# A two-layer fp16 kernel on one core: second-product operations on ScalarE in halves of 384 columns, no kept x sums, new orders

## The chip, the core and the metric

The kernel runs on one core of a Trainium2 chip. TensorE (PE) multiplies, VectorE (DVE) and ScalarE (ACT) do element-wise work and move results out of the PSUM banks, GpSimd (POOL) and SyncE (SP) issue most of the DMA transfers, and TensorE's weight loads (PEld) run beside its matmuls. The metric is the device time of one execution in microseconds. Lower is better. The kernel before was timed three times: 878.06, 879.29 and 879.67 us.

## The reference

```python
# x: 16 x 512 x 768, w1: 768 x 3072, b1: 3072, w2: 3072 x 768, all float32
y = np.matmul(x, w1) + b1
y = np.maximum(y, 0)
return np.matmul(y, w2).astype(np.float32)
```

As one matrix, x has 8192 rows. The two products are 8192 x 768 by 768 x 3072 and 8192 x 3072 by 3072 x 768.

## The kernel before

**Tiling.** The work is cut into 16 iterations: two chunks of the hidden dimension (1536 columns of w1, 1536 rows of w2) times eight blocks of 1024 rows of x. Iterations 0 to 7 go through the blocks with the first chunk and write their results to the output, iterations 8 to 15 go through them again with the second chunk and add to it. `SECOND_CHUNK` gives the order of blocks in the second pass.

**Bilinear products.** Both products are done by a scheme like Strassen's. Instead of all block products of the plain scheme, sums and differences of blocks are multiplied, and sums of the results give the output. Products are fp16 with fp32 sums in PSUM. In each iteration the first product (`add_first`, TensorE line L1013) is 40 products of six matmuls of 128x128 by 128x256, the second product (`add_second`, L1142) 26 products of six matmuls of 128x128 by 128x384. Iteration 0 computes its first product plainly (`first_block`, L923). The operands that are sums are made on DVE: sums of x at L768, of w1 at L784, of w2 at L802, of y (the hidden layer) at L986. The tables at the head of the file (`X_SUMS`, `SECOND_OPS`, ...) say which.

**Banks and operations.** A second product fills a pair of PSUM banks, 384 columns in each. Its six matmuls are three steps h for each of two banks j, with j as the inner loop, so that they alternate between the banks. An *operation* then takes the pair on, for one of three ends. A *seed* writes it, with a sign, into another pair of banks, where later products add to it, a *sum* keeps it in SBUF, and an *out* is a finished piece of output. Operations that add a kept sum run on DVE (L1159, and L1056, L1059, L1064 in the first product), those that only copy or negate run on ScalarE (L1153, and L1049, L1053 in the first product), one instruction of 128x768 each in the second product.

**Slots.** Kept sums and outs lie in nine SBUF slots, called s in the profile. The slot of an out becomes free when its store has landed. Stores go out plainly on SyncE (L1189) in the first chunk and accumulating on GpSimd (L1191) in the second. An out that adds a kept sum can be *apart*: the sum is stored by itself (L1194), ScalarE alone copies the product's part, and the store of that part accumulates on GpSimd. `SPLIT` names outs that are apart in every iteration, `APART` iterations in which all are.

**x and the weights.** GpSimd loads x with a cast to fp16 (xn, L648), ScalarE squares it for a check of ranges (L708), SyncE transposes it by DMA (L700, the *turns*, eight for each block), and DVE makes the sums of x. Block 2 is kept (`KEPT`): in iteration 2 its x and sums are also stored to DRAM (xd, SyncE L721, 20 transfers of 192 KB), and in iteration 8 they are loaded from there for iteration 9 (L728), which needs no turns and no sums of x. The second chunk's weights are cast to DRAM by GpSimd in iterations 2 to 6 (w1d L627, w2d L633), 18 transfers, and loaded by SyncE in iteration 7 (L1363, L1403); the sums of w1 and w2 for the second chunk follow.

**What sets the order.** `plan` adds all of this as tasks with an engine, a cost in ns and dependencies. `Graph.run`, a list scheduler, gives each engine its order from these costs, from latencies between engines (`CROSS`) and from due times that TensorE's product order sets (`FIRST_ORDER`, `SWITCH_ORDER` for iterations 7 and 8, `SECOND_ORDER`, `LAST_ORDER`). Each engine then runs its instructions in that order, and waits at each for what it reads and for the place that it writes.

Of the kernel before, what the change touches and what calls it, by code (L numbers as in the profile page):

```python
# [31 lines left out]
X_SUMS = ((15, 2, 1, -1), (21, 7, 1, -1), (16, 1, 0, -1), (9, 6, 5, -1), (20, 7, 5, -1), (12, 2,  # L32
    0, -1), (14, 3, 5, -1), (11, 2, 5, -1), (8, 4, 5, -1), (17, 6, 1, -1), (10, 3, 1, -1), (22, 6,
    7, -1), (23, 4, 6, -1), (13, 0, 6, -1), (18, 3, 2, -1), (19, 4, 2, -1))
FIRST_U = (8, 9, 21, 18, 2, 13, 20, 19, 1, 14, 10, 17, 11, 22, 6, 12, 5, 23, 15, 16)
W1_SUMS = ((7, 0, 1, 1), (6, 2, 5, 1), (9, 6, 3, -1), (12, 9, 0, -1), (14, 7, 9, -1), (11, 5, 4,
    -1), (8, 6, 4, -1), (13, 7, 2, -1), (10, 8, 7, -1), (15, 3, 5, -1), (16, 3, 10, -1), (17, 1,
# [31 lines left out]
FIRST_ORDER = (16, 0, 12, 36, 20, 8, 4, 7, 9, 1, 18, 24, 3, 15, 10, 28, 32, 38, 6, 21, 14, 35, 17,  # L69
    30, 11, 27, 34, 37, 29, 13, 31, 23, 2, 26, 25, 5, 22, 39, 33, 19)  # L70
SWITCH_ORDER = (16, 0, 12, 36, 20, 4, 9, 8, 7, 18, 24, 3, 1, 10, 15, 28, 21, 38, 6, 14, 32, 35,
    17, 11, 30, 27, 34, 5, 13, 29, 26, 31, 37, 2, 23, 25, 22, 39, 19, 33)

Y_SUMS = ((17, 5, 9, 1), (21, 11, 10, 1), (41, 8, 9, 1), (24, 4, 0, 1), (16, 8, 12, 1), (20, 0, 3,
# [4 lines left out]
SECOND_U = (36, 38, 25, 27, 28, 10, 16, 23, 15, 2, 13, 39, 20, 35, 34, 17, 42, 41, 29, 33, 43, 40,  # L79
    18, 22, 32, 31)  # L80
W2_SUMS = ((11, 2, 1, -1), (9, 7, 6, -1), (14, 9, 3, -1), (8, 1, 5, -1), (20, 9, 5, -1), (17, 3,
    11, 1), (10, 4, 7, -1), (24, 11, 10, -1), (18, 7, 3, -1), (12, 1, 0, -1), (15, 8, 2, -1), (16,
    8, 0, -1), (13, 3, 10, 1), (22, 16, 4, -1), (25, 0, 13, 1), (19, 6, 15, -1), (23, 12, 9, -1),
# [41 lines left out]
    5, 24, 20)  # L125
LAST_ORDER = (13, 15, 4, 17, 10, 8, 12, 18, 3, 0, 1, 2, 14, 19, 23, 21, 11, 16, 25, 7, 9, 5, 22,
    6, 24, 20)
LAST_FOLD = (6,)
LAST_DIRECT = (0, 1, 2, 3, 5)
LAST_POOL = ()  # L130

X_FUSE = (0,)
# [387 lines left out]
SPLIT = (6,)  # L520
# [954 lines left out]
```

## Time and profile before

| | us |
|---|---|
| three runs | 878.06, 879.29, 879.67 |
| profiled execution, own time | 878.07 |
| its span | 876.5 |
| PE busy | 850.6 (97%) |
| DVE busy | 744.5 (85%) |
| ACT busy | 557.8 (64%) |
| POOL busy | 154.7 (18%) |
| DMA, mean rate over the span | 164 GB/s |

The profiled execution lies at the quick end of the three runs. "Busy" is time within instructions, and PE's ends are modelled, since matmuls are pipelined. A window row gives, for a stretch of the span, each engine's busy time and instruction count, the granted TensorE clock (1.00 is full) and the share of the 16 DMA engines' time that transfers took, which can exceed 1. In rows of groups, the figures after the bar are the total busy time, the mean ns of one, and the engine's idle time just before them with what ended most of it. In rows of waits they are total us, count and the longest. In rows of the timeline they are start, duration, engine, line and operation, with the idle time before it and what ended that in brackets.

### The profile page before, as it was taken

To read this page: it belongs to the slowest core of one execution; us is meant where nothing else is said; L and a number is where in the kernel's file an instruction comes from. 1 tells how busy PE (TensorE), PEld (TensorE's weight loads), DVE (VectorE), ACT (ScalarE), POOL (GpSimd) and SP (SyncE) were. 2 spreads that over 40 slices of the span, in tenths; PEclk is the share of its full clock that TensorE was granted. 3 is DMA by queue.
4 is the path that set the end of the run, shared out by engine and by line. 5 is a ranking of instruction groups with operands and counts; after the bars stand their busy time and mean duration, and the time that the engine had idled before them with its cause. 6 is when DMAs were issued, how large, how long until landed. Compare 5 with 4: busy or idle time off the path is not lost. (4 is left out here: it accounts for less than half of the span.)

```text
span 876.5 us, 16636 instructions
## 1 busy us (share of the span) xinstructions
PE 850.6 (97%) x6381; PEld 625.0 (71%) x6381; DVE 744.5 (85%) x1206; ACT 557.8 (64%) x1066; POOL 154.7 (18%) x166
## 2 busy tenths in 40 slices
PE   8997998899999999998999999999999999999996
PEld 7556767577685877867677586776858677686873
DVE  5895995888989899897999969899798988989886
ACT  5866775676767676675766348777747667355462
POOL 5212020020200101010030311405032140401301
PEclk9999999999999999999999999999999999999999
DMA  9999679496683959657595564958887895965746
GB/s 212 200 196 204 145 153 270 84 238 106 152 171 72 220 91 195 113 125 218 162 232 166 85 107 72 202 83 146 146 134 124 153 145 98 145 111 64 127 108 146
DMA packets 166550, 129.71 MB, mean 148 GB/s; under 512 B 87852, under 2 KB 164932, under 8 KB 166468
## 3 DMA queue, kind: packets, MB, share of 16 engines
q0 software_dynamic: 53872, 64.89, 46.8%
q1 hardware_dynamic: 112128, 62.74, 28.4%
q8 instruction: 50, 0.82, 0.4%
q10 hardware_dynamic: 468, 1.00, 0.3%
q14 instruction: 32, 0.26, 0.1%
HBM read 73.54 MB, written 69.99 MB: 164 GB/s over the span
## 5 line engine op out<-in xcount | busy, mean ns | idle before, releaser
L1142 PE MATMUL ps<-v,y 128*128 128x384 f16 x2496 | 416.8, 326 | 2.3 <-ACT ps L1153 0.7
L1013 PE MATMUL ps<-x,v 128*128 128x256 f16 x3600 | 398.1, 273 | 14.0 <-ACT ps L1049 4.1
L1013 PEld LDWEIGHTS <-v 128*128 128x128 f16 x3600 | 352.1, 98 | 59.0 <-issue 16.7
L1142 PEld LDWEIGHTS <-y 128*128 128x128 f16 x2496 | 243.7, 98 | 171.4 <-issue 15.0
L986 DVE TENSOR_TENSOR y<-y 128x768 f16<-128x768 f16 (+1 forms) x368 | 222.4, 639 | 6.6 <-DVE y L1056 0.5
L1056 DVE CUSTOM_DVE_ANT_0 y<-ps,s 128x512 f16<-128x512 f32 x240 | 160.1, 687 | 37.0 <-ACT s L1053 15.9
L1153 ACT ACTIVATE s<-ps 128x768 f32<-128x768 f32 x171 | 138.4, 810 | 81.7 <-PE ps L1142 65.3
L1053 ACT ACTIVATE s<-ps,bt 128x256 f32<-128x256 f32 x180 | 74.8, 473 | 81.5 <-PE ps L1013 72.2
L1191 POOL DMA_DIRECT2D out_dram<-s x79 | 95.5, 1419 | 141.6 <-ACT s L1153 62.7
L768 DVE TENSOR_TENSOR x<-x 128x768 f16<-128x768 f16 (+1 forms) x195 | 108.1, 577 | 9.2 <-DMA x<-xn 8.0
L1053 ACT ACTIVATE y<-ps,bt 128x256 f16<-128x256 f32 x180 | 72.1, 475 | 46.8 <-PE ps L1013 46.7
L1153 ACT ACTIVATE ps<-ps 128x768 f32<-128x768 f32 x80 | 63.6, 795 | 58.9 <-DVE s L1159 35.7
L648 POOL DMA_DIRECT2D xn<-in_x_dram x28 | 21.6, 775 | 395.5 <-ACT xn L708 294.5
L1159 DVE TENSOR_TENSOR s<-ps,s 128x768 f32<-128x768 f32 x85 | 80.4, 954 | 10.4 <-PE ps L1142 8.0
L1159 DVE TENSOR_TENSOR s<-s,ps 128x768 f32<-128x768 f32 x59 | 56.2, 953 | 10.8 <-PE ps L1142 6.8
L708 ACT ACTIVATE xn<-xn 128x768 f16<-128x768 f16 x64 | 53.3, 835 | 0.0
L1049 ACT ACTIVATE ps<-ps 128x512 f32<-128x512 f32 x60 | 35.6, 593 | 9.4 <-DVE y L1056 5.7
L1194 POOL DMA_DIRECT2D out_dram<-s x8 | 9.6, 1197 | 161.0 <-ACT s L1153 161.0
L1064 DVE TENSOR_TENSOR s<-s,ps 128x512 f32<-128x512 f32 x30 | 20.5, 682 | 14.7 <-PE ps L1013 13.4
L923 PE MATMUL ps<-x,v 128*128 128x256 f16 (+1 forms) x216 | 31.9, 308 | 0.7 <-DVE x L873 0.7
L1064 DVE TENSOR_TENSOR ps<-s,ps 128x512 f32<-128x512 f32 x30 | 20.8, 695 | 12.3 <-PE ps L1013 9.1
L784 DVE TENSOR_TENSOR v<-v 128x768 f16<-128x768 f16 x48 | 24.7, 552 | 6.9 <-DMA v<-w1d 3.7
(58 smaller groups left out, 307.9 us busy)
## 6 DMA issues: line engine op xcount, KB each, us to landing
out_dram<-s POOLq DMA_DIRECT2D x87, 384.0 KB, 7.9
out_dram<-s SPq DMA_DIRECT2D x68, 384.0 KB, 9.2
xn<-in_x_dram POOLq DMA_DIRECT2D x26, 768.0 KB, 9.7
xd<-x SPq DMA_DIRECT2D x20, 192.0 KB, 9.3
x<-xd SPq DMA_DIRECT2D x20, 192.0 KB, 3.4
v<-in_w_dram POOLq DMA_DIRECT2D x6, 384.0 KB, 10.6
v<-in_w_dram POOLq DMA_DIRECT2D x12, 192.0 KB, 9.1
w1d<-in_w_dram POOLq DMA_DIRECT2D x6, 384.0 KB, 19.3
```

Of the source, the lines that this page charges most:

```text
L708: self.nc.scalar.activation(out=self.xn[:, s, :], in_=self.xn[:, s, :], func=ACTF.Square, accum_out=self.stat[:, self.stat_at["x"] + i:][: ...
L768: self.nc.vector.tensor_tensor(out=self.two(x, out), in0=self.two(x, in0), in1=self.two(x, in1), op=ALU.add if sign > 0 else ALU.subtract)
L986: self.nc.vector.tensor_tensor(out=self.two(self.y, out), in0=self.two(self.y, in0), in1=self.two(self.y, in1), op=ALU.add if sign > 0 els ...
L1013: nc.tensor.matmul(self.ps[:, at, j * self.QM:(j + 1) * self.QM], lhsT=self.v1[:, gi, self.w1s[c][gi][FIRST_V[p]], k, j * P:(j + 1) * P], ...
L1049: nc.scalar.activation(out=out, in_=ps, scale=float(a), func=func if kind == "out" else ACTF.Copy)
L1053: nc.scalar.activation(out=out[:, j], in_=ps[:, j], func=func, scale=float(a), bias=beta(j))
L1056: nc.vector._custom_dve(TENSOR_ADD_SAT, out=out, in0=ps, in1=s, s0=F_MAX, s1=0.0)
L1064: nc.vector.tensor_tensor(out=out, in0=in0, in1=in1, op=ALU.add if a == b else ALU.subtract)
L1142: nc.tensor.matmul(self.ps[:, bank[ch].at[j], 0:NH], lhsT=self.y[:, ys[SECOND_U[p]], m0:m0 + P], rhs=self.v2[:, slot[SECOND_V[p]], h, :], ...
L1153: nc.scalar.activation(out=out, in_=ps, func=ACTF.Copy, scale=float(a))
L1159: engine.tensor_tensor(out=out, in0=in0, in1=in1, op=ALU.add if a == b else ALU.subtract)
L1191: nc.gpsimd.dma_start(out=rows, in_=out, accum_op=ALU.add)
```

## The change

The operations of ScalarE that `HALVES` names are issued as two instructions of 384 columns, one for each bank of the pair. These are ten of the second product's operations. The second product's six matmuls go bank by bank. No block is kept, so that iteration 9 turns its x and makes its sums like the others; the second pass takes the blocks in the order 7, 0, 1, 2, .... No iteration has all its outs apart, but t1 joins t6 as an out that is apart in every iteration. The casts of the second chunk's weights move from `iteration` to `iteration_end`. The planner has other latencies, an overlap of successive instructions (`OVER`), a queue for transfers (`dma`, `SHARE`, `LAND`) and an earlier release for halves (`early`). All tables of orders are new, no two sums of x are fused into one instruction, and other pairs of y's are. The number of matmuls is the same.

```diff
-SECOND_ORDER = (13, 15, 4, 17, 10, 8, 18, 12, 3, 0, 1, 14, 2, 19, 23, 21, 11, 16, 25, 7, 9, 22, 6,
+SECOND_ORDER = (13, 15, 4, 17, 10, 8, 12, 18, 3, 0, 1, 2, 14, 19, 23, 21, 11, 25, 16, 22, 7, 9, 6,
...
-LAST_FOLD = (6,)
-LAST_DIRECT = (0, 1, 2, 3, 5)
+LAST_FOLD = (5, 6)
+LAST_DIRECT = (0, 1, 2, 3, 5, 7)
...
-X_FUSE = (0,)
-Y_FUSE = (7, 10, 12, 19, 25)
+X_FUSE = ()
+Y_FUSE = (0, 8, 17, 20, 24)
...
-    CROSS = {"PE": 0.15, "DVE": 0.08, "ACT": 0.08, "POOL": 0.1, "SP": 0.1}
+    CROSS = {"PE": 0.25, "DVE": 0.14, "ACT": 0.16, "POOL": 0.1, "SP": 0.1}
+
+    OVER = {"PE": 0.0, "DVE": 0.08, "ACT": 0.1, "POOL": 0.0, "SP": 0.0}
+    SHARE = {"SP": 1 / 3, "POOL": 2 / 3}
+    LAND = {"SP": 2.2, "POOL": 2.0}
...
-SPLIT = (6,)
-APART = (0, 7)
-
-KEPT = (2,)
-SECOND_CHUNK = (7, 2, 0, 1, 3, 4, 5, 6)
+SPLIT = (1, 6)
+APART = ()
+
+HALVES = (2, 8, 12, 13, 19, 20, 21, 22, 23, 24)
+
+KEPT = ()
+SECOND_CHUNK = (7, 0, 1, 2, 3, 4, 5, 6)
...
         def product(p, ch, start):
-            hj = [(h, j) for h in range(3) for j in range(2)]
-            if final and p == order[-1]:
-                hj.sort(key=lambda q: q[1])
-            for h, j in hj:
+            for j, h in ((j, h) for j in range(2) for h in range(3)):
...
                 alone = u is None or (kind == "out" and t in apart)
+                if alone and t in HALVES:
+                    for j in range(2):
+                        combine(nc.scalar, out[:, j], ps[:, j], a, None, None)
+                    return
...
-        if 2 <= it <= 6:
+
+    def iteration_end(self, it):
+
+        g, NSB, NIT = self.g, self.NSB, self.NIT
+        if it + 1 == NIT:
+            self.add_priors(it)
+        begun = g.last_pe
+        self.add_second(it)
+        if 2 <= it <= min(6, NSB - 1):
             for n in range((it - 2) * 4, min((it - 1) * 4, 18)):
                 gi, h = divmod(n, 3)
                 if n < 6:
                     g.add("POOL", 850, lambda gi=gi, h=h: self.load_strip(self.w1dram, 1, gi, h),
-                          writes=[("w1d", gi, h)], lat=9.0, after=[g.last_pe])
+                          writes=[("w1d", gi, h)], lat=15.0, after=[begun], dma=3.2)
                 else:
                     q, h = divmod(n - 6, 3)
                     g.add("POOL", 850, lambda h=h, q=q: self.load_w2(self.w2dram, 1, h, q),
-                          writes=[("w2d", h, q)], lat=9.0, after=[g.last_pe])
-
-    def iteration_end(self, it):
-
-        g, NSB, NIT = self.g, self.NSB, self.NIT
-        if it + 1 == NIT:
-            self.add_priors(it)
-        self.add_second(it)
+                          writes=[("w2d", h, q)], lat=15.0, after=[begun], dma=1.5)
```

Three places of the order that comes out. The first is ScalarE at the start of an early second product (iteration 1). Here ps is a pair of PSUM banks and s a slot, so that a row with ps on the left is a seed. Before:

```order
L1153 ACTIVATE ps<-ps 128x2x384
L1153 ACTIVATE s<-ps 128x768
L1153 ACTIVATE ps<-ps 128x2x384
L1153 ACTIVATE s<-ps 128x768 x3
L708 ACTIVATE xn,stat<-xn 128x768
L1153 ACTIVATE s<-ps 128x768
```

and now:

```order
L1202 ACTIVATE ps<-ps 128x384 x2
L1202 ACTIVATE s<-ps 128x768
L1202 ACTIVATE ps<-ps 128x384 x2
L1202 ACTIVATE s<-ps 128x384 x2
L760 ACTIVATE xn,stat<-xn 128x768
L1202 ACTIVATE s<-ps 128x384 x4
```

The seeds and three of the sums are two instructions each, with one bank in each, in the same places of the queue.

The second place is SyncE's queue in iterations 0 to 2: turns of x (L700, now L752), sums that are stored apart (L1194, now L1247), outs (L1189, now L1242), and x and its sums kept in DRAM (L721). Before:

```order
L700 DMA_TRANSPOSE x<-xn 128x6x128 x8
L1194 DMA out_dram<-s 128x2x384 x7
L1189 DMA out_dram<-s 128x2x384
L700 DMA_TRANSPOSE x<-xn 128x6x128 x8
L721 DMA xd<-x 128x768 x6
L1194 DMA out_dram<-s 128x2x384
L721 DMA xd<-x 128x768 x2
L1189 DMA out_dram<-s 128x2x384 x2
L721 DMA xd<-x 128x768 x2
L1189 DMA out_dram<-s 128x2x384
```

and now:

```order
L752 DMA_TRANSPOSE x<-xn 128x6x128 x8
L1247 DMA out_dram<-s 128x2x384 x2
L1242 DMA out_dram<-s 128x2x384 x6
L752 DMA_TRANSPOSE x<-xn 128x6x128 x8
L1247 DMA out_dram<-s 128x2x384 x2
L1242 DMA out_dram<-s 128x2x384 x6
```

Iteration 0 stores two sums apart where it stored seven, and the stores of x and its sums among the second turns and the outs are gone. On GpSimd's queue the first four casts of w1 still stand behind an x load, but that load is now issued near the end of iteration 2's first product, where it was issued in iteration 1's second product.

The third place is DVE from the end of iteration 8's second product into iteration 9: operations with a kept sum (L1159, now L1208), sums of w2 (L802, now L854), of y (L986, now L1038) and of x (now L820), then the first operations of the first product (L1056 and L1059, now L1108 and L1111). Before:

```order
L1159 TENSOR_TENSOR s<-ps,s 128x768
L802 TENSOR_TENSOR v_66<-v_66 128x1152 x2
L1159 TENSOR_TENSOR s<-ps,s 128x768
L986 TENSOR_TENSOR y<-y 128x768
L1159 TENSOR_TENSOR s<-s,ps 128x768
L986 TENSOR_TENSOR y<-y 128x768
L1159 TENSOR_TENSOR s<-ps,s 128x768 x2
L1056 ISA y<-ps,s 128x2x256 x2
```

and now:

```order
L854 TENSOR_TENSOR v_66<-v_66 128x1152 x3
L1208 TENSOR_TENSOR s<-ps,s 128x768
L1208 TENSOR_TENSOR s<-s,ps 128x768
L1038 TENSOR_TENSOR y<-y 128x768
L820 TENSOR_TENSOR x<-x 128x768
L1208 TENSOR_TENSOR s<-ps,s 128x768
L820 TENSOR_TENSOR x<-x 128x768 x6
L1108 ISA y<-ps,s 128x2x256 x2
L1111 SCALAR_TENSOR_TENSOR s<-ps,bt,s 128x256 x2
L820 TENSOR_TENSOR x<-x 128x768 x3
```

The sums of x that iteration 9 did not need before stand among and behind the last operations of iteration 8.

More of the change, by code (lines that the diff above doesn't have):

```diff
@@ L278 @@
     __slots__ = ("n", "engine", "ns", "fn", "deps", "succ", "regs", "due", "lat", "waits", "ready",
-                 "end", "start", "pe", "idle", "late")
+                 "end", "start", "pe", "idle", "late", "dma", "early")
 class Graph:
@@ L1280, in add_second @@
             writes = [dest]
[L1281 to L1282 removed]
+            split = engine == "ACT" and n in HALVES and n not in folds
+            self.g.add(engine, 850 if split else 810 if engine == "ACT" else 955,
+                       lambda t=n, dest=dest: operation(t, dest), reads=reads, writes=writes,
+                       early=0.37 if split else 0)
             if what == "out":
```

138 lines of the change are left out of this document (89 added, 49 removed), and 8 rows, old and new, of the table Y_SUMS.

## The prediction, as put on record before the changed kernel ran

> **What bounds the kernel now.** I read the page first, then a table of windows with one row per product, then the timeline inside the rows that are too long. The page says that TensorE is the bound over the whole span, at full granted clock:
>
> ```profile
> span 876.5 us, 16636 instructions
> PE 850.6 (97%) x6381; PEld 625.0 (71%) x6381; DVE 744.5 (85%) x1206; ACT 557.8 (64%) x1066; POOL 154.7 (18%) x166
> L1142 PE MATMUL ps<-v,y 128*128 128x384 f16 x2496 | 416.8, 326 | 2.3 <-ACT ps L1153 0.7
> L1013 PE MATMUL ps<-x,v 128*128 128x256 f16 x3600 | 398.1, 273 | 14.0 <-ACT ps L1049 4.1
> ```
>
> The change leaves the number of matmuls alone, so all it can save is time in which TensorE waits. The 16 idle us beside L1013 and L1142 are not all of that: a matmul that waits while the one before it is still modelled as busy shows nothing. The windows show it, because equal work has unequal length. Every product phase is 240 matmuls (first product, L1013) or 156 (second product, L1142):
>
> ```profile
> core 0: us, PE busy (x) PEld busy (x) DVE busy (x) ACT busy (x) POOL busy (x), PEclk, DMA share, GB/s
> 68.70:99.90 31.20, 26.66 (x241) 23.44 (x240) 19.21 (x34) 20.48 (x45) 4.80 (x4) 1.00 0.79 152
> 125.90:158.50 32.60, 26.86 (x242) 23.49 (x241) 21.12 (x38) 18.38 (x42) 0.80 (x1) 1.00 1.19 256
> 158.50:184.90 26.40, 25.81 (x158) 15.21 (x156) 24.25 (x37) 19.66 (x33) 5.58 (x7) 1.00 0.53 108
> 289.20:315.40 26.20, 26.20 (x242) 23.49 (x241) 22.28 (x40) 17.52 (x44) 0.00 (x0) 1.00 0.85 185
> 315.40:341.20 25.80, 25.80 (x159) 15.21 (x157) 23.52 (x35) 19.75 (x34) 4.16 (x5) 1.00 0.57 95
> 393.20:422.90 29.70, 26.73 (x243) 23.49 (x241) 24.06 (x44) 17.22 (x38) 0.00 (x0) 1.00 0.57 178
> 422.90:448.90 26.00, 25.98 (x159) 15.24 (x157) 25.21 (x43) 21.47 (x32) 5.31 (x5) 1.00 0.86 232
> 448.90:475.80 26.90, 26.52 (x242) 23.47 (x241) 23.99 (x40) 14.69 (x34) 3.19 (x3) 1.00 0.88 215
> 475.80:502.80 27.00, 26.21 (x158) 15.12 (x156) 24.57 (x36) 12.92 (x17) 7.19 (x7) 1.00 0.49 76
> 502.80:529.00 26.20, 26.20 (x242) 23.46 (x240) 18.52 (x32) 13.96 (x34) 3.64 (x3) 1.00 0.74 116
> 842.80:876.50 33.70, 26.22 (x158) 15.10 (x155) 25.52 (x35) 11.63 (x15) 4.80 (x4) 0.95 0.56 127
> ```
>
> An undisturbed first product takes 26.20 us (289.20) and a second product 25.80 (315.40). The reader is to see three groups above that: iterations 1 and 2 (31.20, 32.60, then 26.40), and the switch of weight chunks in iterations 7 and 8 (29.70, 26.00, 26.90, 27.00). A fourth loss is inside every 25.80. Weight loads of a second product follow each other evenly until, after twelve of them (two products), there is a short stop:
>
> ```profile
> 265.42 1.88 PEld L1142 LDWEIGHTS <-y 128*128 128x128 f16 x12 [0.20 <-issue]
> 267.50 1.88 PEld L1142 LDWEIGHTS <-y 128*128 128x128 f16 x12 [0.20 <-issue]
> 275.30:287.30 12.00, 12.00 (x76) 7.23 (x74) 1.00 0.63 100
> PEld L1142 <- issue: 15.0, 68, 0.8
> 266.65 0.80 ACT L1153 ACTIVATE ps<-ps 128x768 f32<-128x768 f32 x1 [0.35 <-PE ps L1142]
> ```
>
> The third row is the second half of the same phase, without stops, counted for L1142 alone: 74 loads in 12.00 us, 0.1622 each. Twelve take 1.95 us, but the stretch from 265.42 to 267.50 is 2.08: 0.13 lost. The row of waits counts 68 stops in the kernel, four for each of 16 second products and four more. The last row is what is waited for: ScalarE seeds a pair of banks in one operation of 0.80 us, which begins when the whole product before is done, with only one other product (6 × 0.1622 = 0.97 us) to cover it.
>
> **The change, term by term.** All sums go against the profiled execution, 878.07 us (span 876.5 and 1.57 around it); it is the quick end of the three runs, 1.22 under their median of 879.29, so I add 1.2 at the end.
>
> **A: halves of 384 columns, bank by bank.** Before, the way from the end of a product to the next use of the seeded banks is 0.97 + 0.13 = 1.10 us, of which 0.80 is the operation and 0.30 the two handovers. Now bank 0 is finished after three matmuls, 0.49 us before the product ends, and its half can begin there. For one half the trace has these neighbours:
>
> ```profile
> L830 ACT ACTIVATE junk<-v 128x384 f16<-128x384 f16 x16 | 8.4, 525 | 0.2
> L1049 ACT ACTIVATE ps<-ps 128x512 f32<-128x512 f32 x60 | 35.6, 593 | 9.4 <-DVE y L1056 5.7
> 868.49 1.14 PE L1142 MATMUL ps<-v,y 128*128 128x384 f16 x6 [0.18 <-DVE s L1159]
> ```
>
> A half cannot cost less than 0.40 (half of the undivided 0.80) nor more than the 0.593 of 512 columns; I take 0.525, the row of the same width. Counted from the product's end, bank 0 is seeded at −0.49 + 0.15 + 0.525 + 0.15 = 0.34 and bank 1 at 0.15 + 0.525 + 0.15 = 0.83 us; TensorE wants them at 0.97 and 1.46. At 0.593 the second is 0.90: no wait at either bound. The bank-by-bank order costs TensorE nothing by the last row, the final product of before, already issued that way: six matmuls take 1.14 us, and five starts of 0.1622 with one modelled matmul of 0.326 are 1.14. So the whole stop goes: 25.80 − 156 × 0.1622 = 0.50 per second product, 7.5 for 15 of them, and 0.2 of the last, whose order is its own: **−7.7**. Bounds: −8.8 (68 × 0.13), and a loss where the two halves bind each other (a rival below).
> The price on ScalarE is 160 split operations. A pair costs between 0.80 (no overhead) and 1.19, by 525 ns at most 1.05: 160 × 0.25 = 40 us at most, hidden in ScalarE's idle 319 us (876.5 − 557.8); in a second product it is busy 19.75 of 25.80 and gets ten pairs, 2.5 us more, 22.3. Without that cover it would be 2.5 us per second product. [...]
>
> **B: iterations 1 and 2.** What TensorE waits for in iteration 1:
>
> ```profile
> 70.03 0.81 ACT L1153 ACTIVATE s<-ps 128x768 f32<-128x768 f32 x1 [1.66 <-DMA out_dram<-s]
> 70.89 1.47 PE L1013 MATMUL ps<-x,v 128*128 128x256 f16 x12 [0.72 <-ACT s L1153]
> 73.83 2.12 PE L1013 MATMUL ps<-x,v 128*128 128x256 f16 x18 [1.47 <-ACT s L1153]
> 78.31 0.92 PE L1013 MATMUL ps<-x,v 128*128 128x256 f16 x7 [2.35 <-ACT ps L1049]
> out_dram<-s SPq DMA_DIRECT2D x8, 384.0 KB, 10.9
> ```
>
> ScalarE cannot write a slot of s until an earlier store of that slot has landed; the banks behind it stay full and TensorE stands. The last row is SyncE's stores of iteration 0's second product (42.9 to 68.7): iteration 0 stored seven sums apart on SyncE and accumulated the seven outputs behind them on GpSimd, 14 stores for 7. With APART empty it stores ten times instead of fifteen. In iteration 2 there are two causes:
>
> ```profile
> 155.95 0.56 DVE L768 TENSOR_TENSOR x<-x 128x768 f16<-128x768 f16 x1 [4.48 <-DMA x<-xn]
> 157.16 1.47 PE L1013 MATMUL ps<-x,v 128*128 128x256 f16 x12 [2.49 <-DVE y L1056]
> out_dram<-s SPq DMA_DIRECT2D x4, 384.0 KB, 12.7
> 123.45 3.25 POOL L627 DMA_DIRECT2D w1d<-in_w_dram  x4
> w1d<-in_w_dram POOLq DMA_DIRECT2D x1, 384.0 KB, 28.7
> xd<-x SPq DMA_DIRECT2D x20, 192.0 KB, 9.3
> ACT s L1053 <- DMA out_dram<-s: 8.9, 3, 3.8
> ```
>
> In this phase the DMA engines are full (share 1.19): 20 stores of x and of its sums (3.8 MB) go out on SyncE among the outputs and the transposes, and beside them run the four casts of w1 that GpSimd issued at 123.45; the one that the window counts took 28.7 us. Stores land after 12.7 us, and ScalarE waits (last row; these three are all that this line has in the kernel); the transposes come late, and DVE, waiting 4.48 us for them, lets its queue of relus stand behind it. Both loads go: the 20 stores are out, and the casts now go out behind the x load near the end of this first product, about 26 us later, when only the usual outputs and turns are on the queues. Iteration 9 pays by eight transposes on SyncE (as all others do) in place of 20 loads. Saved: 31.20 − 26.20 = 5.0, 32.60 − 26.20 = 6.4 and 26.40 − 25.80 = 0.6, together 12.0; I keep 0.5 for the casts: **−11.5**. Bounds: nothing, and 12.0.
>
> **C: the switch (iterations 7 and 8).**
>
> ```profile
> 408.76 0.56 DVE L784 TENSOR_TENSOR v<-v 128x768 f16<-128x768 f16 x1 [3.67 <-DMA v<-w1d]
> 496.26 2.11 PE L1142 MATMUL ps<-v,y 128*128 128x384 f16 x12 [0.39 <-DVE v L802]
> L768 DVE TENSOR_TENSOR x<-x 128x768 f16<-128x768 f16 x182 | 95.9, 550 | 9.2 <-DMA x<-xn 8.0 <-DVE x L768 0.3
> L1159 DVE TENSOR_TENSOR s<-ps,s 128x768 f32<-128x768 f32 x85 | 80.4, 954 | 10.4 <-PE ps L1142 8.0 <-ACT s L1153 0.9
> ```
>
> DVE stands 3.67 us at a sum of w1 whose load is late, and later works off the sums of w2. The excess is 3.5 + 0.2 + 0.7 + 1.2 = 5.6. The new orders put the sums of w1 behind other work, so the first 3.5 should go. But iteration 9 now needs 16 sums of x that it used to load: 16 × 0.550 = 8.8 us on DVE between 475.8 and 529.0, where it is idle 53.2 − 43.1 = 10.1 us. The output t1, which ScalarE now copies in iterations 8 and 9 as elsewhere, takes 2 × 0.954 off DVE (last row): 6.9 us more in 10.1 of idle time, from which goes the 1.7 by which the two phases are to shrink (53.2 − 26.2 − 25.3). That leaves 1.5 us, which is little, since the sums are due at set products, so I leave 1.5 us of stops: **−4.1**. Bounds: −5.6, and, if none of the idle time can be used, +3.4 (6.9 lost, 3.5 gained in iteration 7, the other stops as they were).
>
> t1's split costs one more store per iteration (a sum held until it lands), and APART and KEPT give back more than that early. The tail behind the last matmul I leave.
>
> Sum: 878.1 − 7.7 − 11.5 − 4.1 = 854.8; against the median 1.2 more, **856.0**. With all of A, B and C gone it is 878.1 − 25.3 = 852.8 by the profile's own time.
>
> **Rivals.**
> *The switch overloads DVE.* For it: only 1.5 us of slack, in a phase where DVE already holds TensorE up (496.26). Against: the whole excess there is 1.2 us, so DVE is behind only briefly. Then C ends at its upper bound: 856.0 + 4.1 + 3.4 = 863.5.
> *Stores and turns stay late in iterations 1 and 2.* For it: casts and x loads are moved, not removed, and everything shares what the share column counts; iteration 0 still runs at full DMA with the first weights. Against: 3.8 MB and five stores are really gone. If all of B stays: 867.5. [...]
> *Halves bind each other.* If ScalarE starts bank 0 only when all six matmuls are done and TensorE restarts only when both banks are seeded, the way is 0.30 + 1.05 − 0.97 = 0.38 lost instead of 0.13: 64 × 0.25 = 16 us more than before and none of A, 856 + 7.7 + 16 = 880: no change. With one of the two releases by bank, the stop is gone all the same. Against: the two banks are separate operands, and the new order puts two products between where the operation is undivided.
> *Slower: slots bind everywhere.* Each iteration now holds one sum more until its store lands, in the same nine slots, and ScalarE takes over an output that waits for a slot. If every first product met the three waits of iteration 1 (0.72 + 1.47 + 2.35 = 4.5 us), 14 iterations would cost 63: 919. It decides from 23.3 / 14 = 1.7 us per iteration. Against: after iteration 2 these waits end, and the DMA share is 0.57 in a second product.
>
> **How the numbers follow.** Forecast 0.73 (852.5 to 861), the switch 0.10 (863.5), late stores 0.09 (867.5), halves bind 0.03 (880), slots bind 0.03 (919), and 0.02 for no visible effect. A measurement of this kernel tells about 0.2% (1.8 us) from no change. Faster is 0.73 + 0.10 + 0.09 = 0.92, the same 0.03 + 0.02 = 0.05, slower 0.03. The range, 852 to 868, holds the first three cases.
>
> **What would show it.** A right: second products of 25.3 us, and no stop after twelve weight loads. B right: 26.2 for the first products of iterations 1 and 2, no wait of ScalarE for stores. C right: iteration 7's first product near 26.2, iterations 8 and 9 together under 2 us above 26.2 + 25.3. Wrong: waits for stores in iterations 3 and later, ScalarE busy over 24 of 25.3 us in a second product, or DVE waiting for transposes.

## The result and the profile after

The changed kernel takes 854.92 us (median of four runs, 854.47 to 855.49) against 879.40 us (four runs, 878.06 to 879.67). The ratio is 0.9725, with a 95% interval of 0.9708 to 0.9742. The forecast was 856.0.

The page of the changed kernel, from the same parts as the lines shown of before:

```profile
span 853.9 us, 16777 instructions
PE 841.3 (99%) x6381; PEld 625.2 (73%) x6381; DVE 741.9 (87%) x1233; ACT 563.7 (66%) x1229; POOL 158.6 (19%) x170
L1191 PE MATMUL ps<-v,y 128*128 128x384 f16 x2496 | 408.9, 326 | 1.3 <-DVE v L854 0.7
L1065 PE MATMUL ps<-x,v 128*128 128x256 f16 x3600 | 396.4, 273 | 2.2 <-ACT ps L1105 1.4
out_dram<-s SPq DMA_DIRECT2D x69, 384.0 KB, 3.3
```

The count of matmuls is the same, and the idle time ahead of the two matmul lines fell from 16.3 to 3.5 us. SyncE's stores land after 3.3 us (the median in the last row) instead of 9.2 (the same row of the page before). The windows of the changed kernel, one product each, with the columns of the prediction's table: iteration 1 first, 2 first and second, 5 second, 7 first and second, 8 first and second, 9 first, 15 second with the end.

```profile
68.20:95.70 27.50, 26.31 (x241) 23.42 (x240) 22.20 (x40) 23.11 (x53) 1.98 (x2) 1.00 0.72 139
121.10:147.50 26.40, 26.32 (x241) 23.46 (x240) 19.82 (x35) 23.20 (x53) 5.28 (x6) 1.00 0.66 120
147.50:172.90 25.40, 25.40 (x159) 15.30 (x158) 24.74 (x40) 15.24 (x33) 1.98 (x2) 1.00 1.11 216
302.80:328.10 25.30, 25.30 (x158) 15.23 (x156) 24.80 (x40) 15.17 (x33) 2.00 (x2) 1.00 0.93 189
379.70:405.90 26.20, 26.20 (x242) 23.45 (x241) 21.01 (x38) 17.42 (x39) 1.21 (x1) 1.00 0.51 142
405.90:431.30 25.40, 25.40 (x159) 15.28 (x157) 25.02 (x41) 18.30 (x39) 1.20 (x1) 1.00 0.66 192
431.30:457.60 26.30, 26.30 (x241) 23.43 (x240) 25.99 (x46) 18.61 (x44) 1.97 (x2) 1.00 0.67 128
457.60:483.80 26.20, 25.52 (x158) 15.26 (x157) 26.01 (x39) 15.23 (x33) 9.14 (x8) 1.00 0.81 119
483.80:510.00 26.20, 26.20 (x242) 23.48 (x240) 24.10 (x46) 18.57 (x44) 4.41 (x4) 1.00 0.97 148
821.60:853.90 32.30, 25.47 (x158) 15.13 (x155) 25.77 (x37) 13.90 (x27) 3.57 (x3) 0.94 0.56 135
```

Second products take 25.3 (25.80 before). Iteration 1's first product is at 27.50 (31.20), iteration 2's at 26.40 (32.60), iteration 7's at 26.20 (29.70). Iteration 8's second product, at 26.20, is the only one of the switch that still waits for long. DVE is busy 26.01 of these 26.20 us.

The start of iteration 4's second product in the timeline, weight loads and the first seed:

```profile
251.11 7.84 PEld L1191 LDWEIGHTS <-y 128*128 128x128 f16 x49
252.44 0.95 ACT L1202 ACTIVATE ps<-ps 128x384 f32<-128x384 f32 x2
```

The table of waits over the whole kernel has this row for the loads of second products:

```profile
PEld L1191 <- issue: 0.9, 1, 0.9
```

and the groups by line and shape have these for the halves, into a slot and into banks:

```profile
L1202 ACT ACTIVATE s<-ps 128x384 f32<-128x384 f32 x190 | 86.8, 495 | 46.9 <-PE ps L1191 46.9
L1202 ACT ACTIVATE ps<-ps 128x384 f32<-128x384 f32 x128 | 55.9, 484 | 5.2 <-DVE s L1208 3.3 <-PE ps L1191 0.5
```

The loads run on without the stop after every twelve. The row of stops says 0.9 us in one wait, where it was 15.0 us in 68. (The same table has new, smaller stops of these loads behind DVE's sums of y, 3.6 us in 12, where there were 0.2 us in one.) A half takes 484 or 495 ns, and the pair shown takes 0.95 us.

### The profile page after: what moved, and what is told of

It reads as the page before. It is cut to its first block, busy times and chain, and to the rows that moved or that the text cites. A ratio compares the mean times of both kernels' runs of the same rounds, so it can differ in the third digit from the quotient of the medians.

```text
span 853.9 us, 16777 instructions
## 1 busy us (share of the span) xinstructions
PE 841.3 (99%) x6381; PEld 625.2 (73%) x6381; DVE 741.9 (87%) x1233; ACT 563.7 (66%) x1229; POOL 158.6 (19%) x170
## 4 chain that ended last, share of the span: by engine, by line
PE 90%; DVE 4%; DMA 3%; ACT 1%; issue 1%; SPq 0%; DVEq 0%; POOLq 0%
PE ps L1191 45%; PE ps L1065 41%; PE ps L975 4%; DMA x<-xn 2%; DVE y L1038 1%; DMA v<-in_w_dram 1%; DVE s L1208 1%; DVE v L854 1%; ACT xn L760 1%; DVE y L1108 1%; ACT ps L1105 0%; SPq L752 0%; ACT y L1105 0%; DVE ps L1208 0%; PE ps L917 0%
## 5 line engine op out<-in xcount | busy, mean ns | idle before, releaser
L1191 PE MATMUL ps<-v,y 128*128 128x384 f16 x2496 | 408.9, 326 | 1.3 <-DVE v L854 0.7
L1065 PEld LDWEIGHTS <-v 128*128 128x128 f16 x3600 | 352.2, 98 | 45.3 <-issue 3.1
L1202 ACT ACTIVATE s<-ps 128x384 f32<-128x384 f32 (+1 forms) x270 | 150.1, 589 | 114.7 <-PE ps L1191 114.0
L1038 DVE TENSOR_TENSOR y<-y 128x768 f16<-128x768 f16 (+1 forms) x368 | 218.6, 640 | 2.8
L1108 DVE CUSTOM_DVE_ANT_0 y<-ps,s 128x512 f16<-128x512 f32 x240 | 158.1, 687 | 64.5 <-PE ps L1065 52.7
L1244 POOL DMA_DIRECT2D out_dram<-s x74 | 89.4, 1479 | 241.3 <-ACT s L1202 184.6
L820 DVE TENSOR_TENSOR x<-x 128x768 f16<-128x768 f16 x224 | 114.4, 553 | 8.6 <-DMA x<-xn 5.7
L1202 ACT ACTIVATE ps<-ps 128x384 f32<-128x384 f32 (+1 forms) x144 | 68.6, 518 | 54.7 <-PE ps L1191 50.0
L700 POOL DMA_DIRECT2D xn<-in_x_dram x30 | 23.4, 783 | 337.9 <-ACT xn L760 199.5
L1208 DVE TENSOR_TENSOR s<-ps,s 128x768 f32<-128x768 f32 x77 | 72.5, 953 | 2.0 <-PE ps L1191 1.5
L1208 DVE TENSOR_TENSOR s<-s,ps 128x768 f32<-128x768 f32 x63 | 59.8, 950 | 1.6
L1105 ACT ACTIVATE ps<-ps,bt 128x256 f32<-128x256 f32 x60 | 26.7, 444 | 19.3 <-PE ps L1065 13.7
L1247 POOL DMA_DIRECT2D out_dram<-s x15 | 18.9, 1258 | 92.4 <-ACT s L1202 78.8
L975 PEld LDWEIGHTS <-v 128*128 128x128 f16 x216 | 20.9, 98 | 11.1 <-DMA v<-in_w_dram 0.6
```

The costliest lines, as they stand in the source:

```text
L820: self.nc.vector.tensor_tensor(out=self.two(x, out), in0=self.two(x, in0), in1=self.two(x, in1), op=ALU.add if sign > 0 else ALU.subtract)
L975: nc.tensor.matmul(self.ps[:, ps.at[0], cols], lhsT=self.v1[:, gi, 2 * h + k2, k, j * P:(j + 1) * P], rhs=rhs, start=(k2 == 0 and k == 0), ...
L1038: self.nc.vector.tensor_tensor(out=self.two(self.y, out), in0=self.two(self.y, in0), in1=self.two(self.y, in1), op=ALU.add if sign > 0 els ...
L1065: nc.tensor.matmul(self.ps[:, at, j * self.QM:(j + 1) * self.QM], lhsT=self.v1[:, gi, self.w1s[c][gi][FIRST_V[p]], k, j * P:(j + 1) * P], ...
L1105: nc.scalar.activation(out=out[:, j], in_=ps[:, j], func=func, scale=float(a), bias=beta(j))
L1108: nc.vector._custom_dve(TENSOR_ADD_SAT, out=out, in0=ps, in1=s, s0=F_MAX, s1=0.0)
```

## Experiments on the halves

The theory was that ScalarE's seed is the last step ahead of TensorE's stop, and that halves take it away because the first can begin before the product ends. The rivals were the new order of products and the order of the banks. Four kernels tell them apart, two taken from the changed kernel and two from the kernel before. Here and below, kernels of different rounds are compared through the kernel before, whose median lies at 878.8 to 879.5 us in all of them.

**One operation again, in the changed kernel.**

```diff
-                if alone and t in HALVES:
+                if False:
```

> The changed kernel, with its order, but each of ScalarE's ten operations undivided again (one instruction of 768 columns). Theory A (halves let ScalarE begin before the product ends): where one product lies between, the way is 0.80 + 0.30 = 1.10 us against 0.97 of cover, so four stops of 0.13 come back in each of 16 second products: 854.9 + 8 = 863, second products of 25.8 us. Rival (the new order of products and the bank-by-bank matmuls did it): 855.

Measured: 865.9 us, 11.0 more. The row of stops is back:

```profile
PEld L1191 <- issue: 15.5, 77, 0.9
```

So the halves carry the gain. It cost 11 us and not 8: there are 77 stops where the old order had 68, some 10 us at 0.13 each, and the last 1 us is not traced. For these stops the new order alone, without the halves, is no better than the old one.

**The banks in turn again, in the changed kernel.**

```diff
-            for j, h in ((j, h) for j in range(2) for h in range(3)):
+            hj = [(h, j) for h in range(3) for j in range(2)]
+            if final and p == order[-1]:
+                hj.sort(key=lambda q: q[1])
+            for h, j in hj:
```

> The changed kernel with halves, but the six matmuls of a second product alternate between the two banks as before, so that bank 0 is done only 0.16 us before the product ends. Theory A: the first half begins at the product's end, the second 0.43 later; bank 1 is seeded at 0.15 + 0.43 + 0.525 + 0.15 = 1.25 us and wanted at 0.97 + 0.16 = 1.13, so about 0.12 is lost per seed, 64 times: 854.9 + 7.7 = 862 to 863. Rival (halves alone do it, the order of the banks does not matter): 855.

Measured: 855.81 us (855.46 to 856.83). The rival was nearly right:

```profile
PEld L1194 <- issue: 2.6, 10, 0.9
```

Ten stops come back, not 64. My working (0.43 + 0.525 us for a pair of halves, where the pair shown above takes 0.95) let the first half begin at the product's end, though in this order bank 0 is done one matmul, 0.16 us, earlier. By that estimate the second bank is ready at 1.25 − 0.16 = 1.09 us and wanted at 1.13, which fits but was not traced operation by operation. The bank-by-bank order is worth less than 1 us; the halves do the rest.

**Halves and bank order alone, in the kernel before.**

```diff
+HALVES = (2, 8, 12, 13, 19, 20, 21, 22, 23, 24)
...
-            for h, j in hj:
+            for j, h in ((j, h) for j in range(2) for h in range(3)):
...
+                if alone and t in HALVES:
+                    for j in range(2):
+                        combine(nc.scalar, out[:, j], ps[:, j], a, None, None)
+                    return
```

> The kernel before, with its tables, planner and orders, and only the halves and the bank-by-bank matmuls put in. Theory A: second products of 25.3 us, 879.4 - 7.7 = 871.7; the stalls of iterations 1, 2, 7 and 8 stay. Rival (it needs the new order): stays near 879; rival (ScalarE's longer queue costs time): above 880.

Measured: 874.35 us, ratio 0.9946 (0.9925 to 0.9966). About 5 us of the 7.7 came. The stops and iteration 1's first product in its profile:

```profile
PEld L1140 <- issue: 3.9, 16, 0.8
68.40:101.60 33.20, 27.88 (x241) 23.98 (x240) 19.50 (x35) 21.33 (x47) 5.52 (x5) 0.95 0.78 149
```

The stops fell from 15.0 us to 3.9 without any new order. Iteration 1's first product is 2.0 us longer than in the profile before, at a granted clock of 0.95. The last section comes back to this clock, which the halves do not explain.

**The bank order alone, in the kernel before.** The edit is the second piece of the diff above.

> The kernel before with the bank-by-bank matmuls alone, ScalarE's operations undivided. Theory A: an undivided operation still waits for the whole product and frees both banks at once, so the stops stay: 879.4, second products of 25.8 us. Rival (the order of the matmuls is the gain): 872; rival (three matmuls in a row on one bank are slower): above 881.

Measured: 877.49 us, ratio 0.9988 (0.9972 to 1.0004): no difference that can be measured.

```profile
PEld L1139 <- issue: 14.3, 68, 0.7
```

All 68 stops are there. So in this kernel bank by bank neither helps nor costs while an operation takes both banks at once.

## Experiments on iterations 1 and 2: parts of the change in the kernel before

The theory was that fewer stores in iteration 0 and no kept x free iterations 1 and 2, and the casts a little. Each part was put into the kernel before by itself, and the order planned anew by its own planner.

**No iteration apart.**

```diff
-APART = (0, 7)
+APART = ()
```

> The kernel before with no iteration whose outs are all stored apart (APART empty), the orders planned anew by its own planner. Theory B: iteration 0's 15 stores become 9, the three waits for store landings in iteration 1's first product go (31.2 to about 26.5), iterations 2, 7 and 8 stay: 879.4 - 4.7 = 874.7. Rival (iteration 1 waits for the weights and x still arriving, not for the stores): 879; rival (DVE, which takes over the six outs, becomes late): above 880.

Measured: 881.52 us, ratio 1.0026 (1.0010 to 1.0042), slower by 0.3%. Iterations 1 and 7 (first product) and 8 (first and second):

```profile
68.80:97.20 28.40, 26.60 (x241) 23.32 (x240) 24.87 (x46) 18.13 (x42) 0.00 (x0) 1.00 0.35 85
391.20:424.10 32.90, 29.47 (x241) 24.74 (x240) 24.05 (x44) 17.30 (x38) 0.00 (x0) 0.90 0.53 166
449.90:478.50 28.60, 27.11 (x243) 23.40 (x241) 25.68 (x45) 13.95 (x32) 0.00 (x0) 1.00 0.55 171
478.50:508.20 29.70, 26.80 (x159) 14.99 (x157) 28.84 (x43) 12.93 (x17) 7.24 (x7) 1.00 0.44 67
```

Iteration 1 gained 2.8 of its 5.0 us. Iteration 8 lost 1.7 and 2.7 us: in its second product DVE is now busy 28.84 of 29.70 us, 4.3 us more than before, with the work that iteration 7's outs apart had kept off it just ahead of the sums of w2: in iteration 7's second product DVE now spends 8.3 us on operations with a kept sum instead of 3.8, and the sums of the weights are pushed back. I had priced APART by its stores alone; iteration 7's half of it was relief for DVE. Iteration 7 lost 3.2 us as well, but its clock was at 0.50 for 6.8 us (mean 0.90), which alone costs 3.4 by estimate, half of the 6.8 (last section).

**No kept block.**

```diff
-KEPT = (2,)
-SECOND_CHUNK = (7, 2, 0, 1, 3, 4, 5, 6)
+KEPT = ()
+SECOND_CHUNK = (7, 0, 1, 2, 3, 4, 5, 6)
```

> The kernel before with no block kept (KEPT empty, second pass in the order 7, 0, 1, ...), planned anew by its own planner; the four casts of w1 stay ahead of iteration 2. Theory B: the 3.8 MB of x on SyncE among outs and turns are the larger part of iteration 2's 6.4 us, the casts the smaller; 4 of the 6.4 go, iteration 9's sums of x cost up to 2: 875 to 877. Rival (the casts are the cause): iteration 2 stays at 32.6, 879 to 881.

Measured: 876.75 us, ratio 0.9972 (0.9956 to 0.9988). Iteration 2's first product and iteration 9's:

```profile
127.50:153.70 26.20, 26.20 (x242) 23.48 (x241) 22.06 (x40) 18.29 (x42) 0.79 (x1) 1.00 1.10 213
496.90:528.70 31.80, 28.28 (x242) 24.10 (x240) 25.75 (x45) 14.08 (x34) 3.62 (x3) 0.95 0.66 109
```

All of iteration 2's 6.4 us went, with the casts still ahead of it and the DMA share still at 1.10. So neither a full DMA share nor the casts were the cause by themselves; with the 20 transfers of x gone the loss is gone. Whether it was their place in SyncE's queue or their bytes, this run does not tell. Iteration 9 then lost 5.6 us, by estimate some 1.7 of them to the clock (0.95 in its window; last section) and the rest since its sums of x fall on a DVE with little room: it is busy 25.75 us there, 18.52 before. That is the rival of the switch, in the old order.

**Both.**

```diff
-APART = (0, 7)
+APART = ()
...
-KEPT = (2,)
-SECOND_CHUNK = (7, 2, 0, 1, 3, 4, 5, 6)
+KEPT = ()
+SECOND_CHUNK = (7, 0, 1, 2, 3, 4, 5, 6)
```

> The kernel before with APART and KEPT both empty, planned anew by its own planner. Theory B: the two act on different iterations and add: 879.4 - 4.7 - 3.5 = about 871. Rival (they share one backlog of transfers, so that either alone removes most): the gain is clearly less than the sum of the two runs alone.

Measured: 878.62 us, ratio 0.9991 (0.9978 to 1.0004), no change. The windows of iteration 1's first product, iteration 8's second and iteration 9's first:

```profile
68.70:97.20 28.50, 26.70 (x242) 23.39 (x241) 25.01 (x46) 18.18 (x42) 0.00 (x0) 1.00 0.36 87
469.50:499.20 29.70, 26.80 (x158) 15.00 (x157) 29.23 (x45) 17.13 (x29) 8.86 (x9) 1.00 0.82 128
499.20:529.40 30.20, 26.68 (x242) 23.38 (x240) 25.54 (x45) 13.98 (x34) 3.62 (x3) 1.00 0.64 98
```

and the timeline of iteration 1 has as its longest wait of TensorE:

```profile
79.51 17.73 PE L1013 MATMUL ps<-x,v 128*128 128x256 f16 x161 [1.25 <-DVE x L768]
```

The early gain is there in full, 2.7 + 6.4 us, and the switch gives all of it back: 2.7 in iteration 8's second product, 4.0 in iteration 9, and 1.9 and 1.6 in the first products of iterations 7 (at a clock of 0.95) and 8. Iteration 1 no longer waits for stores but for DVE, which took the six outs.

**The casts moved.**

```diff
-        if 2 <= it <= 6:
+
+    def iteration_end(self, it):
...
+        begun = g.last_pe
+        self.add_second(it)
+        if 2 <= it <= 6:
             for n in range((it - 2) * 4, min((it - 1) * 4, 18)):
...
-                          writes=[("w1d", gi, h)], lat=9.0, after=[g.last_pe])
+                          writes=[("w1d", gi, h)], lat=9.0, after=[begun])
...
-                          writes=[("w2d", h, q)], lat=9.0, after=[g.last_pe])
+                          writes=[("w2d", h, q)], lat=9.0, after=[begun])
```

> The kernel before with only the weight casts moved to where the change puts them in the code, planned anew by its own planner. Theory B: x's 20 stores still fill the queues, so iteration 2 gets shorter by no more than 2 us: 877.5 to 879.5. Rival (the casts are the cause of iteration 2's stalls): iteration 2's first product falls to 27 us or less, 874.

Measured: 879.43 us, ratio 0.9994 (0.9977 to 1.0010). The casts in GpSimd's timeline, and iterations 1 and 2, first products:

```profile
124.89 3.25 POOL L627 DMA_DIRECT2D w1d<-in_w_dram  x4
68.90:101.50 32.60, 28.32 (x241) 24.23 (x240) 19.47 (x35) 20.49 (x45) 4.80 (x4) 0.95 0.78 147
127.30:160.90 33.60, 28.12 (x243) 24.05 (x241) 22.38 (x40) 18.73 (x42) 0.84 (x2) 0.95 1.17 254
```

The edit moved nothing. The four casts still go out 2.4 us ahead of iteration 2's first product (124.89 against 127.30), as in the kernel before (123.45 against 125.90), and in the traces every engine of the two kernels has the same instructions in the same order. So this run says nothing about the casts, and whether they add to the stall while x is kept stays untested. What is shown is that they do not stall iteration 2 without it: in the run with no kept block they went out at 125.04, 2.5 us ahead of a first product of 26.20 us. This run is instead a second profile of the order of before, and shows its spread: iterations 1 and 2 at 32.60 and 33.60 us with a clock of 0.95, where the first profile has 31.20 and 32.60 at 1.00.

These runs leave a question. The early gain of KEPT and APART is real, and in the old kernel the switch takes it back. What keeps the switch free in the changed kernel?

## Experiments on the switch: parts taken out of the changed kernel

**The old tables.** The ten tables of orders and fusions (X_SUMS, W1_SUMS, W2_SUMS, Y_SUMS, FIRST_ORDER, SWITCH_ORDER, SECOND_ORDER, LAST_ORDER, X_FUSE, Y_FUSE) from before, all else as changed.

```diff
-X_FUSE = ()
-Y_FUSE = (0, 8, 17, 20, 24)
+X_FUSE = (0,)
+Y_FUSE = (7, 10, 12, 19, 25)
...
```

> The changed kernel with the ten old tables of orders and fusions (X_SUMS, W1_SUMS, W2_SUMS, Y_SUMS, FIRST_ORDER, SWITCH_ORDER, SECOND_ORDER, LAST_ORDER, X_FUSE, Y_FUSE), all else as changed. Theory C-tables (the new orders keep the switch free): the stalls of iterations 7 to 9 come back, 5 us or more: 860 to 870. Rival C-planner (the planner's costs and latencies, or the output moved to ScalarE, keep it free): 855 to 857.

Measured: 859.39 us (859.23 to 860.58), 4.5 more. Iterations 8 and 9, first products:

```profile
431.30:458.80 27.50, 26.63 (x242) 23.46 (x241) 27.16 (x48) 17.34 (x40) 1.20 (x1) 1.00 0.39 84
484.20:511.50 27.30, 26.52 (x242) 23.47 (x240) 24.00 (x44) 15.66 (x38) 3.89 (x4) 1.00 0.77 121
```

1.2 and 1.1 us come back here, and with the second products (iteration 8's 0.8 shorter, iteration 9's 1.3 longer) 2.8 in all. The total lies between what the theory (860 or more) and its rival (857 or less) had expected. The tables help, but do not carry the switch.

**t1 back on DVE.**

```diff
-SPLIT = (1, 6)
+SPLIT = (6,)
```

> The changed kernel with SPLIT (6,) again: output t1 back on VectorE, 0.95 us per iteration more there, one store and one ScalarE operation per iteration fewer. Theory C as predicted (1.5 us of slack on VectorE in iterations 8 and 9): 2 us lost there and nothing elsewhere, 857. Rival (VectorE has slack): 855. Rival (VectorE is near its limit in every iteration): over 860.

Measured: 857.69 us (856.20 to 857.96), 2.8 more. Iteration 8's second product and iteration 9's first:

```profile
458.40:485.30 26.90, 25.68 (x158) 15.19 (x157) 26.66 (x40) 15.23 (x33) 7.97 (x7) 1.00 0.70 103
485.30:512.90 27.60, 26.35 (x242) 23.46 (x240) 24.96 (x47) 17.85 (x43) 4.42 (x5) 1.00 0.88 139
```

0.7 + 1.4 = 2.1 us are in the two phases where I had expected 2. This part was priced rightly. "Nothing elsewhere" was not: iteration 14's first product lost another 0.9 (27.10 us in its window).

**The old planner.** Its latencies and its lack of the three new parts come back; the costs in ns of the tasks stay as changed.

```diff
-    CROSS = {"PE": 0.25, "DVE": 0.14, "ACT": 0.16, "POOL": 0.1, "SP": 0.1}
+    CROSS = {"PE": 0.15, "DVE": 0.08, "ACT": 0.08, "POOL": 0.1, "SP": 0.1}
-    OVER = {"PE": 0.0, "DVE": 0.08, "ACT": 0.1, "POOL": 0.0, "SP": 0.0}
+    OVER = {"PE": 0.0, "DVE": 0.0, "ACT": 0.0, "POOL": 0.0, "SP": 0.0}
-        t.succ, t.ready, t.end, t.start, t.dma, t.early = [], 0.0, None, None, dma, early
+        t.succ, t.ready, t.end, t.start, t.dma, t.early = [], 0.0, None, None, 0.0, 0.0
```

> The changed kernel planned with the old latencies between engines, no overlap of successive instructions, no queue of transfers and no early release of halves, so that only the order of instructions changes. Theory C-tables: 855 to 857, since the tables carry the order. Rival C-planner: stalls in iterations 7 to 9 and in 1, over 860.

Measured: 870.67 us (869.66 to 873.31), 15.7 more. My theory of the tables falls, and the rival holds. The windows of iteration 8's second product and of iteration 9's and 10's first:

```profile
459.70:489.70 30.00, 26.31 (x158) 14.80 (x156) 29.72 (x45) 16.68 (x36) 9.96 (x9) 1.00 0.75 115
489.70:518.30 28.60, 26.71 (x242) 23.48 (x240) 25.19 (x47) 18.31 (x43) 4.41 (x5) 1.00 0.87 139
543.60:571.90 28.30, 26.61 (x243) 23.50 (x241) 21.26 (x38) 20.66 (x45) 4.49 (x5) 1.00 0.92 142
```

The only long wait of TensorE inside the last of them, from the timeline:

```profile
554.50 3.44 PE L1065 MATMUL ps<-x,v 128*128 128x256 f16 x30 [1.51 <-DVE ps L1116]
```

Iterations 8 and 9 lose 3.8 and 2.4 us, and each of the first products of 10 to 13 some 2 us at one seed that DVE makes late, with DVE idle for 7 us of the phase. The instructions are the same. Only their order differs, as it comes out when the planner is told shorter latencies and no overlap, queue of transfers or early release. So what keeps iterations 8 and 9 free is above all the planner's picture of the engines: 6.2 us of the 15.7 are lost there, and about 7.4 in iterations 10 to 13. The runs did not try latencies, overlap, transfer queue and early release singly; which of the four matters most stays open.

Iteration 7 is another matter. Its first product stays at 26.2 to 26.7 us in all three runs and at 29 or more in the six that start from the kernel before, so that it is freed by something that these three share, which no run took out alone. The traces show where it lies. These are the waits of SyncE's queue in the first 15 us of the phase, before and in the changed kernel, and the changed kernel's first sum of w1 there:

```profile
SPq L1363 <- DMA out_dram<-s: 3.1, 4, 1.3
SPq L1419 <- PE ps L1065: 6.7, 11, 2.2
389.77 0.55 DVE L836 TENSOR_TENSOR v<-v 128x768 f16<-128x768 f16 x1
```

Before, SyncE's loads of w1 stood behind the landing of stores (and 2.4 us behind a load of x), and DVE then stood 3.67 us at the first sum, which began 15.6 us into the phase. Now these loads wait only until TensorE has done with the old weights, and the first sum begins 10.1 us into the phase without a wait. Which edit brought the loads forward stays open.

## A version beyond the change

In the changed kernel the chain of work that ended last goes, in iterations 1 to 4, through transposes of x and ScalarE's squares; here a square of iteration 1 from the timeline:

```profile
88.53 0.84 ACT L760 ACTIVATE xn<-xn 128x768 f16<-128x768 f16 x1 [1.26 <-DMA x<-xn]
```

and a piece of the chain in iteration 2:

```profile
141.07 1.01 ACT xn L760 x3
```

A square writes over xn, so it must wait until the transposes have read xn, and a seed for TensorE stands behind three squares. Written to a scratch tile, a square need not wait.

```diff
-            self.nc.scalar.activation(out=self.xn[:, s, :], in_=self.xn[:, s, :],
+            self.nc.scalar.activation(out=self.junk, in_=self.xn[:, s, :],
...
-        self.g.add("ACT", 930, square, writes=[("xn", s), ("stat", "x", i)], due=due, idle=True)
+        self.g.add("ACT", 1035, square, reads=[("xn", s)], writes=["junk", ("stat", "x", i)], due=due, idle=True)
```

> The changed kernel, but ScalarE's squares of x write to a scratch tile in place of xn, so that they no longer wait for the transposes that read xn, and the planner takes them at 1035 ns in place of 930, so that two and not three stand ahead of the last seed of a first product. If that queue is the cause of the stop at product 33 of iterations 1 to 4 and 8 (1.35 + 0.25 + 0.22 + 0.37 + 0.1 us): these go, 854.9 - 2.2 = 852.7. Rival (the transposes are late for VectorE too, which then waits in ScalarE's place): 855.

Measured: 853.66 us (853.46 to 854.02); the changed kernel's four runs lie at 854.47 to 855.49. Against before the ratio is 0.9707 (0.9670 to 0.9744), an interval that overlaps that of the change, so that the windows and not the ratios show the gain. Iterations 1 and 2, first products, and iteration 12's second:

```profile
68.10:94.30 26.20, 26.20 (x242) 23.45 (x240) 21.38 (x39) 25.01 (x57) 1.98 (x2) 1.00 0.72 135
119.70:145.90 26.20, 26.20 (x242) 23.47 (x241) 19.63 (x35) 25.06 (x58) 3.66 (x4) 1.00 0.68 125
662.80:689.90 27.10, 25.67 (x156) 14.98 (x157) 26.96 (x44) 14.02 (x28) 9.00 (x9) 1.00 0.81 118
```

The stops at product 33 are gone, so the squares took part in them. The edit changes both what a square waits for and where the planner puts it, and does not tell the two apart; in the run with the old tables iteration 1's first product took 26.30 us with the squares in place, so that another order frees it as well. A new stop of 1.8 us in iteration 12, where DVE is busy 26.96 of 27.10, takes back part of the 2.2.

## Why the prediction was right, point by point

- **A, −7.7.** Right in size and cause: 0.5 us in each second product, by halves and not by the order (one operation again: the stops return). The pair costs 0.95 us and is hidden as argued. A slip in the working did no harm: by its own figures ScalarE ends bank 0's half at 0.185 us, so that bank 1 is seeded at 0.86 and not at 0.83, still ahead of 1.46. The part on the order of the banks was beside the point: it is worth less than 1 us, so that a start 0.49 us before the product ends is not needed; by the corrected working above it is enough that TensorE can go on with bank 0 while ScalarE is still at bank 1.
- **The last second product** was given 0.2. With the end of the kernel it went from 33.7 to 32.3, 1.4. The part behind the last matmul is 6.9 and 6.8 us long, so nearly all of the 1.4 lies ahead of it. Halves and bank order alone, in the kernel before, brought the phase to 33.1. The new order, fold and direct outs at the end, which I left unpriced, lie in it too, and no run took them out alone.
- **B, −11.5.** Measured 3.7 + 6.2 + 0.5 (iteration 2's second product without A's share) = 10.4. The 1.1 missing are mostly the stop in iteration 1 that went with the squares. The causes were only half right. Without kept x all of iteration 2's loss is gone, with the casts still ahead of it; the 0.5 that I kept back for the casts no run shows. APART takes away the wait for stores, but alone it leaves a loss of 2.3 us to waits for DVE in its place.
- **C, −4.1.** Measured 3.5 + 0.1 + 0.6 + 0.3 = 4.5 (29.70, 26.00, 26.90 and 27.00 against 26.20, 25.40, 26.30 and 26.20, less A's 0.5 in the two second products), with iteration 9 free. DVE's load was foreseen rightly: 43.1 + 6.9 = 50.0 us in iteration 8's second product and iteration 9's first, measured 26.01 + 24.10 = 50.1. The number of the switch is right too, and its reason is not. "The new orders put the sums of w1 behind other work" is not what frees iteration 7: the sums run earlier, since their loads come earlier, and with the old tables the phase is as good as free (26.7 us). Nor do the tables keep iterations 8 and 9 free: they are worth 2.8 us there, the planner's latencies, overlap, queue of transfers and early release at least 6.2, and these I had not priced at all. In the old planner the rival of the switch, to which I gave 0.10, is what happens: 4.0 to 5.6 us lost in iteration 9 (both parts, and KEPT alone, there with some 1.7 of clock).
- **ScalarE's load.** I expected it at 22.3 of 25.3 us in a second product. It is 15.2, since the planner moved six of a block's eight squares of x into the first product, where it is 23.1.
- **The slower rival**, slots that bind everywhere, did not occur: stores land after 3.3 us on SyncE, and the waits of the changed kernel show ScalarE waiting for no store. One of the signs of being wrong is there in small: DVE still waits for transposes, 5.7 us in six waits (8.0 in six before).
- **The sum.** The profiled executions differ by 876.5 − 853.9 = 22.6 us in span: 7.5 (A in 15 second products) + 10.4 + 4.5 + 1.4 = 23.8, less 1.2 net of small new stops (the largest in iterations 4, 13 and 15). Forecast were 23.3. That B came out 1.1 lower, C 0.4 and the last product 1.2 higher, and that the new stops nearly cancel the rest, is luck. The medians differ by 24.5, because the profiled execution of before lies below its median and that of the changed kernel 0.6 above its own.

## What to carry to other kernels

Here two engines handed a pair of banks back and forth and each waited for the whole of one operation; cutting it at the bank boundary, so that by the working of point A TensorE can go on with the first bank while ScalarE is still at the second, took the stops away (15.0 us before, 0.9 in the changed kernel, 15.5 with one operation again), and the extra instruction (0.95 us a pair against 0.80) was free, since ScalarE had idle time (busy 15.2 of 25.3 us in a second product). A saving at one place is worth only what the next tight place lets through: here no kept x and no outs apart saved 9 us early and lost it at the switch, until the order was planned with other latencies, overlap and a queue of transfers. Price an edit by everything it relieved: the outs apart were stores in iteration 0, and spare time on DVE in iteration 7. And look in the trace whether an edit of a planner's input has moved anything: the casts stayed where they were.

## What the runs showed of the hardware that was not expected

In some stalled phases TensorE's granted clock fell to half, after waits of which none was longer than 3.13 us. In the kernel without a kept block, iteration 9 has three waits within 8 us, of 1.52, 0.75 and 1.25 us. These are TensorE's timeline from the first wait on, and the windows around the last:

```profile
503.19 3.45 PE L1013 MATMUL ps<-x,v 128*128 128x256 f16 x30 [1.52 <-DVE x L768]
507.39 0.81 PE L1013 MATMUL ps<-x,v 128*128 128x256 f16 x6 [0.75 <-DVE x L768]
509.45 19.45 PE L1013 MATMUL ps<-x,v 128*128 128x256 f16 x162 [1.25 <-DVE x L768]
506.30:509.40 3.10, 1.15 (x10) 0.73 (x8) 2.77 (x6) 0.00 (x0) 0.00 (x0) 0.99 0.98 170
509.45:512.75 3.30, 3.30 (x16) 2.30 (x16) 2.62 (x6) 1.38 (x4) 0.00 (x0) 0.50 0.01 1
512.75:516.00 3.25, 3.25 (x32) 2.88 (x31) 0.90 (x2) 1.31 (x4) 0.00 (x0) 1.00 0.01 3
```

TensorE is 37% busy for 3.1 us, then runs 16 matmuls in 3.30 us at a clock of 0.50 and 32 in 3.25 us at 1.00. So half of the 3.30 us, some 1.7 by this estimate, is lost on top of the waits. Of the profiles here only five have such bursts ahead of their last matmul, ten in all, nine of them 3.4 us long and one 6.8. All five are of kernels made from the one before, and the bursts lie in stalled phases of iterations 1, 2, 7 or 9: the rows above with a clock of 0.95 or 0.90 are such phases. (The row of 32.30 us with 0.94 is not: there the clock falls behind the last matmul, as in the kernel before.) Nine of the ten have a wait of 2.3 to 3.1 us right ahead; the one shown has the three short ones.

The same waits come with and without a burst. The kernel before waited 0.72, 1.47 and 2.35 us in iteration 1, and none followed; the run whose casts did not move, with the same order, waited 0.64, 1.32 and 2.33, and one did. The run with the bank order alone waited 3.10 us in iteration 2 without one. So in these profiles a stalled phase lost some 1.7 us beyond its waits in some executions and not in others; what sets the clock to half they do not show. A difference of 1.7 us between stalled phases of two profiles need then not be one of the kernels: that holds for the 2.0 us of the run with halves alone, and for iteration 7 of the runs with no outs apart.
